# Other byte offsets for the activation tiles of a hybrid encoder layer

## The chip, the cores and the metric

The kernel runs on one core of one Trainium2 chip. The metric is the time of one execution in microseconds (us). Its work on the engines is told by their names in the profile: PE (TensorE, matmuls), PEld (TensorE's loads of the stationary operand), DVE (VectorE), ACT (ScalarE), POOL (GpSimd) and SP, which only issues transfers here.

## The reference

One encoder layer over 256 tokens of 2048 channels, in float32:

```python
h = rmsnorm(x, norm_mix_pre); z = h @ w_in            # 2048 -> 13312
conv_b, conv_c, conv_in, q, k, v, g_a, g_b = split(z)
y_a = (conv_b * conv3(conv_c * conv_in)) @ w_out_conv
y_b = attention(rope(rmsnorm(q)), rope(rmsnorm(k)), v) @ w_out_attn
mixed = (sigmoid(g_a + bias) * y_a + sigmoid(g_b + bias) * y_b) @ w_merge
x = x + rmsnorm(mixed, norm_mix_post)
h = rmsnorm(x, norm_mlp_pre)                          # then an MLP of 8192 hidden channels
x = x + rmsnorm(square(relu(h @ w_up)) @ w_down, norm_mlp_post)
```

There are 16 query heads and 4 key/value heads of 128 channels, with rotary positions.

## The kernel before, in words

Every float32 product is made of three matmuls: each operand is split into a high and a low float32r part (`split`, lines 74 to 81), and high times high, high times low and low times high are summed in PSUM. The weights come from HBM in pieces of 512 KB (`raw`); ACT writes their high part `whi` (L76), DVE their low part `wlo` (L77).

A layer of work is a matrix of 2048 by 512 weights against all 256 tokens, and it is done in one of two ways. `linear` (L152 to L154) holds 128 tokens as the stationary operand and moves 512 columns of weights: 96 matmuls a layer. `linear_channels` (L182, L186, L189) holds 128 by 128 weights and moves all 256 tokens: 192 matmuls a layer. So one text speaks of tokens that move, and of weights that move.

The split tokens lie in three large tiles of SBUF, each with a high and a low half, and `pair` (line 88) makes them:

- A: first the normalised input `hT` (moves in 12 convolution and 8 gate layers; stationary in the K, the V and 4 Q layers, where the weights move), later the hidden activations `fT` (stationary in the 16 layers of `down`).
- B: first `yT`, the convolution's output (moves in 4 layers), then `mT`, the merged branches (stationary in 4 layers of `merged`).
- C: first `oT`, the attention's output (moves in 4 layers), then `x2T`, the input of the MLP (stationary in the first of 16 `w_up` layers, which `hidden` does; moves in the other 15, `hidden_channels`).

The order is: K, V; four times Q, then three convolution layers with the attention of that group among them; gate A and `w_oc` layers in turn (8), gate B and `w_oa` layers in turn (8); 4 merge layers; and four times 4 layers of `w_up` and 4 of `w_down`. Matmuls are issued in this order on PE and nothing else is reordered by the change. The attention's own matmuls (L386 to L388) and the transposes (L231, L419, L584) are placed among the convolution layers by a list of due times (`later`, `tick`).

`LATE` gives the number of float32 elements by which a role's data start late in its tile; the tile is made longer by the largest of them. The pool `big` holds A, then M (keys and values, then the merged sum), then C, then B, one behind the other, and the weight buffers `raw`, `whi` and `wlo` come behind it. In bytes of a partition, A begins at 18112, M at 50944, C at 67328, B at 100096, `raw` at 133056; every `whi` and `wlo` buffer begins at 192 modulo 256, also those of the second ring that is added after the attention. The pieces that a matmul reads are multiples of 256 bytes apart from their tile's start, so a role has one distance modulo 256, and here it is given as that of the moving operand minus that of the stationary one:

| role | layers | distance before |
|---|---|---|
| A, tokens move (convolution, gates) | 20 | 64 |
| B, tokens move (`w_oc`) | 4 | 64 |
| C, tokens move (`w_oa`, `w_up`) | 4 + 15 | 64 |
| A, weights move (K, V, Q) | 6 | 192 |
| A, weights move (`w_down`) | 16 | 0 |
| B, weights move (merge) | 4 | 0 |
| C, weights move (first `w_up`) | 1 | 192 |

In the attention, scores (keys move against queries) have 64 and values (probabilities move against values) 192.

Of the kernel before, what the change touches and what calls it, by code (L numbers as in the profile page):

```python
# [10 lines left out]
F32R = mybir.dt.float32r  # L11
# [4 lines left out]
P = 128  # L16
# [16 lines left out]
def trunk_kernel(  # L33
# [30 lines left out]
    big = ctx.enter_context(tc.tile_pool(name="big", bufs=1))  # L64
# [18 lines left out]

    LATE = {"A": {True: 16, False: 0}, "B": {True: 0, False: 48}, "C": {True: 0}}

    def pair(tag, moving):

        n, at = 2 * KT * T, LATE[tag][moving]  # L90
        flat = big.tile([P, n + max(LATE[tag].values())], F32R, tag=tag, name=tag)
        both = flat[:, at : at + n].rearrange("p (h k t) -> p h k t", h=2, k=KT)
        return both[:, 0], both[:, 1]

# [181 lines left out]
    g_bias = ch[:, 5:7, :]  # L276

    hT = pair("A", True)

    def first_operands(k, n):  # L280
# [99 lines left out]
    )  # L380

    oT = pair("C", True)
    yT = pair("B", True)

    def mm3(acc, a, b, first, last):
# [363 lines left out]
```

## Time and profile before

| | us |
|---|---|
| median of 3 runs (1607.99 to 1609.61) | 1609.29 |
| the profiled execution, its own time | 1608.78 |
| its span, first to last instruction | 1607.0 |
| PE busy | 1594.8 |
| DVE busy | 948.0 |
| ACT busy | 710.0 |

A matmul's recorded duration overlaps the next one's, since they are pipelined. So the rate of PE is read from how many matmuls start in a stretch of time, and the duration only tells two rates apart. A view by stretches gives the busy time of PE and the number of its instructions; the number counts also those two or three that reach into the stretch at its edges.

### The profile page before, as it was taken

The page shows a single profiled execution, that of the slowest core. Times are in us where ns is not written, and L with a number is a line of the kernel's source. Part 1 is how long each engine was busy: PE and PEld are TensorE (multiplying, and loading weights), DVE is VectorE, ACT ScalarE, POOL GpSimd, SP SyncE. Part 2 cuts the span into 40 slices and gives each one's busy share as a digit, 9 for nine tenths or more (in the row PEclk, how much of TensorE's full clock was granted, in tenths as well). Part 3 has the DMA queues.
Part 4 walks back from the last instruction along what each step waited for, and adds up shares of the span by engine and source line. Part 5 has one row for each costly group of instructions (what it writes and reads, how often), then busy time and mean ns, then how long its engine had stood idle before and what let it go on. Part 6 is the DMA issues. An engine that isn't in the chain of part 4 may idle for free.

```text
span 1607.0 us, 26865 instructions
## 1 busy us (share of the span) xinstructions
PE 1594.8 (99%) x11210; PEld 1485.8 (92%) x11210; DVE 948.0 (59%) x1107; ACT 710.0 (44%) x860; POOL 35.7 (2%) x23
## 2 busy tenths in 40 slices
PE   9999999999999999999999999999999999999997
PEld 7799998999999999999988898899988998899986
DVE  6767676676765554555555865446655565555654
ACT  7444444444454443444444644444433344334441
POOL 0110100101000000000000000000000000000000
PEclk9999999999999999999999999999999999999999
DMA  8655546555476666666765666666666666656662
GB/s 316 199 178 158 184 137 204 173 168 183 152 251 193 192 189 204 191 195 194 247 207 163 200 190 194 197 192 186 183 199 191 188 186 191 192 183 195 186 207 85
DMA packets 86297, 306.28 MB, mean 191 GB/s; under 512 B 9632, under 2 KB 10016, under 8 KB 85920
## 3 DMA queue, kind: packets, MB, share of 16 engines
q1 hardware_dynamic: 84608, 300.32, 59.8%
q10 hardware_dynamic: 1568, 4.25, 0.8%
q8 instruction: 87, 1.43, 0.4%
q14 instruction: 34, 0.28, 0.1%
HBM read 302.44 MB, written 2.10 MB: 190 GB/s over the span
## 4 chain that ended last, share of the span: by engine, by line
PE 98%; DVE 1%; DMA 0%; POOL 0%; issue 0%; ACT 0%; SPq 0%; DVEq 0%; POOLq 0%; ACTq 0%
PE acc L182 20%; PE acc L189 20%; PE acc L186 20%; PE acc L153 12%; PE acc L154 12%; PE acc L152 12%; PE at L386 0%; PE at L387 0%; PE at L388 0%; PE tr L419 0%; DMA raw<-in_w_in 0%; PE tr L231 0%; POOL rs L243 0%; DVE wlo L77 0%; PE tr L584 0%
## 5 line engine op out<-in xcount | busy, mean ns | idle before, releaser
L77 DVE TENSOR_TENSOR wlo<-raw,whi 128x1024 fp32r<-128x1024 f32 (+1 forms) x561 | 684.9, 1223 | 583.9 <-ACT whi L76 582.2
L76 ACT CAST whi<-raw 128x1024 fp32r<-128x1024 f32 (+1 forms) x561 | 588.1, 1050 | 758.4 <-PE acc L186 385.0
L182 PE MATMUL acc<-A,whi 128*128 128x256 f32 x1280 | 357.1, 279 | 0.0
L186 PE MATMUL acc<-A,whi 128*128 128x256 f32 x1280 | 355.2, 278 | 0.0
L189 PE MATMUL acc<-A,wlo 128*128 128x256 f32 x1280 | 355.1, 277 | 0.0
L182 PE MATMUL acc<-C,whi 128*128 128x256 f32 x1216 | 339.5, 279 | 0.0
L189 PE MATMUL acc<-C,wlo 128*128 128x256 f32 x1216 | 338.7, 279 | 0.0
L186 PE MATMUL acc<-C,whi 128*128 128x256 f32 x1216 | 338.5, 278 | 0.0
L152 PE MATMUL acc<-whi,A 128*128 128x512 f32 x704 | 275.3, 392 | 1.7 <-ACT whi L76 1.7
L153 PE MATMUL acc<-wlo,A 128*128 128x512 f32 x704 | 276.1, 392 | 0.8 <-DVE wlo L77 0.8
L154 PE MATMUL acc<-whi,A 128*128 128x512 f32 x704 | 275.8, 392 | 0.0
L186 PEld LDWEIGHTS acc<-A,whi 128*128 128x128 f32 x1280 | 240.4, 188 | 0.2
L182 PEld LDWEIGHTS acc<-A,whi 128*128 128x128 f32 x1280 | 240.3, 188 | 0.2
L189 PEld LDWEIGHTS acc<-A,wlo 128*128 128x128 f32 x1280 | 240.1, 188 | 0.0
L189 PEld LDWEIGHTS acc<-C,wlo 128*128 128x128 f32 x1216 | 228.5, 188 | 0.0
L182 PEld LDWEIGHTS acc<-C,whi 128*128 128x128 f32 x1216 | 228.1, 188 | 0.2
L186 PEld LDWEIGHTS acc<-C,whi 128*128 128x128 f32 x1216 | 227.8, 187 | 0.2
L153 PEld LDWEIGHTS acc<-wlo,A 128*128 128x128 f32 x704 | 132.6, 188 | 30.4 <-DVE wlo L77 2.1
L152 PEld LDWEIGHTS acc<-whi,A 128*128 128x128 f32 x704 | 132.4, 189 | 30.4 <-ACT whi L76 2.5
L154 PEld LDWEIGHTS acc<-whi,A 128*128 128x128 f32 x704 | 132.7, 188 | 28.8
L182 PE MATMUL acc<-B,whi 128*128 128x256 f32 x256 | 70.7, 276 | 0.0
L186 PE MATMUL acc<-B,whi 128*128 128x256 f32 x256 | 70.7, 276 | 0.0
(144 smaller groups left out, 1113.7 us busy)
## 6 DMA issues: line engine op xcount, KB each, us to landing
raw<-in_w_in SPq DMA_DIRECT2D x207, 512.0 KB, 4.3
raw<-in_w_up SPq DMA_DIRECT2D x128, 512.0 KB, 3.6
raw<-in_w_dn SPq DMA_DIRECT2D x128, 512.0 KB, 3.8
raw<-in_w_oc SPq DMA_DIRECT2D x32, 512.0 KB, 4.4
raw<-in_w_oa SPq DMA_DIRECT2D x32, 512.0 KB, 4.2
raw<-in_w_mg SPq DMA_DIRECT2D x32, 512.0 KB, 4.3
xj<-in_x SPq DMA_DIRECT2D x4, 512.0 KB, 8.0
xr<-in_x ACTq DMA_DIRECT2D x1, 2048.0 KB, 9.8
```

Of the source, the lines that this page charges most:

```text
L76: nc.scalar.copy(hi, src)
L77: nc.vector.tensor_tensor(lo, src, hi.bitcast(F32), op=ALU.subtract)
L152: nc.tensor.matmul(accs[t], lhsT=ah[:, a, ts_], rhs=wh[:, g, :], start=first, stop=False)
L153: nc.tensor.matmul(accs[t], lhsT=ah[:, a, ts_], rhs=wl[:, g, :], start=False, stop=False)
L154: nc.tensor.matmul(accs[t], lhsT=al[:, a, ts_], rhs=wh[:, g, :], start=False, stop=last)
L182: nc.tensor.matmul(acc, lhsT=wh[:, g, cs], rhs=ah[:, a, :], start=a == 0 and c % 2 == 0, stop=False, skip_group_check=True,)
L186: nc.tensor.matmul(acc, lhsT=wh[:, g, cs], rhs=al[:, a, :], start=False, stop=False, skip_group_check=True)
L189: nc.tensor.matmul(acc, lhsT=wl[:, g, cs], rhs=ah[:, a, :], start=False, stop=a == KT - 1, skip_group_check=True)
```

## The change

The offsets in `LATE` change, and the size of a tile is rounded up to a multiple of 16 elements (64 bytes). Nothing else is edited.

```diff
-    LATE = {"A": {True: 16, False: 0}, "B": {True: 0, False: 48}, "C": {True: 0}}
+    LATE = {"A": {True: 32, False: 48}, "B": {True: 8, False: 8}, "C": {True: 0}}
...
         n, at = 2 * KT * T, LATE[tag][moving]
-        flat = big.tile([P, n + max(LATE[tag].values())], F32R, tag=tag, name=tag)
+        flat = big.tile([P, n + -(-max(LATE[tag].values()) // 16) * 16], F32R, tag=tag, name=tag)
```

A grows from 32832 to 32960 bytes, so M, C and B begin 128 bytes later; B shrinks from 32960 to 32832, so `raw` and the weight buffers stay where they are. The distances become:

| role | before | after |
|---|---|---|
| A, tokens move | 64 | 128 |
| B, tokens move | 64 | 224 |
| C, tokens move | 64 | 192 |
| A, weights move (K, V, Q) | 192 | 128 |
| A, weights move (`w_down`) | 0 | 64 |
| B, weights move (merge) | 0 | 32 |
| C, weights move (first `w_up`) | 192 | 64 |
| scores / values | 64 / 192 | 192 / 64 |

## Rows read from the trace of the kernel before

**Rows 1.** The page: busy time of the engines, and the chain by engine.

```profile
PE 1594.8 (99%) x11210; PEld 1485.8 (92%) x11210; DVE 948.0 (59%) x1107; ACT 710.0 (44%) x860; POOL 35.7 (2%) x23
...
PE 98%; DVE 1%; DMA 0%; POOL 0%; issue 0%; ACT 0%; SPq 0%; DVEq 0%; POOLq 0%; ACTq 0%
```

**Rows 2.** PE by stretches: start:end, length, busy (count), granted clock, DMA.

```profile
154.40:176.80 22.40, 22.40 (x99) 1.00 0.61 190
176.80:252.00 75.20, 75.20 (x650) 1.00 0.53 168
...
447.40:795.60 348.20, 348.20 (x3074) 1.00 0.65 207
795.60:860.90 65.30, 65.30 (x290) 1.00 0.65 203
885.80:910.10 24.30, 24.30 (x115) 1.00 0.51 163
910.10:978.80 68.70, 68.70 (x585) 1.00 0.69 215
979.00:1066.00 87.00, 87.00 (x386) 1.00 0.64 193
1066.00:1156.30 90.30, 90.30 (x769) 1.00 0.62 187
...
1421.00:1511.30 90.30, 90.30 (x768) 1.00 0.61 187
```

**Rows 3.** Groups of PE matmuls by line, 447.5 to 795: xcount, busy us, mean ns.

```profile
L182 PE MATMUL acc<-A,whi 128*128 128x256 f32 x512 | 141.3, 276 | 0.0
...
L182 PE MATMUL acc<-B,whi 128*128 128x256 f32 x256 | 70.7, 276 | 0.0
...
L182 PE MATMUL acc<-C,whi 128*128 128x256 f32 x255 | 70.4, 276 | 0.0
```

**Rows 4.** The same view, 1066.2 to 1156: w_up layers of the second quarter.

```profile
L189 PE MATMUL acc<-C,wlo 128*128 128x256 f32 x255 | 71.1, 279 | 0.0
L186 PE MATMUL acc<-C,whi 128*128 128x256 f32 x255 | 71.1, 279 | 0.0
L182 PE MATMUL acc<-C,whi 128*128 128x256 f32 x254 | 71.1, 280 | 0.0
```

**Rows 5.** PE in order of time (start us, us): attention values at 220.21.

```profile
220.21 0.29 PE L386 MATMUL at<-ph,kv 128*128 128x256 f32 x1
220.33 0.28 PE L387 MATMUL at<-pl,kv 128*128 128x256 f32 x1
220.45 0.28 PE L388 MATMUL at<-ph,kv 128*128 128x256 f32 x1
220.56 0.28 PE L386 MATMUL at<-ph,kv 128*128 128x256 f32 x1
220.68 0.28 PE L387 MATMUL at<-pl,kv 128*128 128x256 f32 x1
220.79 0.28 PE L388 MATMUL at<-ph,kv 128*128 128x256 f32 x1
220.90 0.28 PE L386 MATMUL at<-kv,qh 128*128 128x256 f32 x1
```

**Rows 6.** The same view: attention values at 122.21.

```profile
122.21 0.28 PE L386 MATMUL at<-ph,kv 128*128 128x256 f32 x1
122.33 0.28 PE L387 MATMUL at<-pl,kv 128*128 128x256 f32 x1
122.45 0.28 PE L388 MATMUL at<-ph,kv 128*128 128x256 f32 x1
122.56 0.28 PE L386 MATMUL at<-ph,kv 128*128 128x256 f32 x1
122.68 0.28 PE L387 MATMUL at<-pl,kv 128*128 128x256 f32 x1
122.80 0.28 PE L388 MATMUL at<-ph,kv 128*128 128x256 f32 x1
```

**Rows 7.** The chain in order of time (start us, us): one group of transposes.

```profile
93.16 0.44 PE tr L231 x4
```

**Rows 8.** PE, PEld, DVE, ACT, POOL by stretches: gate stage, second quarter of w_up.

```profile
447.40:795.60 348.20, 348.20 (x3074) 348.20 (x3074) 189.38 (x179) 156.92 (x173) 0.00 (x0) 1.00 0.65 207
...
1066.00:1156.30 90.30, 90.30 (x769) 90.30 (x768) 50.36 (x52) 37.06 (x40) 0.00 (x0) 1.00 0.62 187
```

## The prediction, made before the result was known

> **What bounds the kernel now.** I read the page first: PE is busy 1594.8 of 1607.0 us, and 98% of the chain is PE [rows 1]. DVE and ACT stand at 59% and 44%. So the time is the number of matmuls times the interval at which PE starts them, and the change touches only the addresses that these matmuls read. The next view is therefore PE by stretches, one stretch for each stage, with the matmuls that the code puts there [rows 2]. I divide length by number.
>
> Where 256 tokens move: the gate stage holds 16 layers of 192, 3072 matmuls in 348.2 us, **113.3 ns** each. A quarter of w_up holds 768 in 90.3 us, **117.6 ns**, a difference of 4.3 ns. Where 512 columns of weights move: four layers of down hold 384 in 87.0 us, **226.6 ns**; three layers of merge 288 in 65.3 us, 226.7 ns; but one Q layer holds 96 in 22.4 us, **233.3 ns**. The granted clock is 1.00 of 2.4 GHz in all of these, so it is not the clock. The views by line say the same with durations: 276 ns for A, B and C in the gate stage [rows 3], 279 to 280 ns for C in w_up [rows 4].
>
> What the reader should see is that there are two rhythms for each kind of layer, about 4% and 3% apart, and that they are held for whole stages. For weights that move, the two go with the distance: 0 (down, merge) is the quicker, 192 (Q) the slower. For tokens that move, the distance is 64 throughout, and both rhythms occur; even the same tile C is quick against w_oa and slow against w_up. So at 64 the distance doesn't decide it; what came before does. The stage that begins behind a layer with moving weights (convolution behind Q, w_up behind down) begins slow, and the gate stage, which follows a convolution that had already gone over, stays quick for 3072 matmuls.
>
> One place shows tokens-sized matmuls at another distance: the attention's values, at 192, in 16 blocks of 6. In 12 of them the starts go as at 220.21: intervals of 0.12, 0.12, and then 0.11, 0.12, 0.11, 0.11, and what follows is quick [rows 5]. In 4 of them they stay at 0.12 all through, as at 122.21 [rows 6]. At 192 a slow beginning is thus mostly left within two matmuls, whereas w_up at 64 keeps it for 768.
>
> **The change part by part.** No instruction, transfer or wait is added or taken; the list of PE, ACT, DVE and SP is the same. All of the effect is an interval times a count. The price of a rhythm: 4.3 ns x 192 = 0.83 us for a layer of moving tokens, (233.3 - 226.6) x 96 = 0.64 us for one of moving weights.
>
> 1. *C, tokens move, w_up: 64 to 192.* 15 layers, 2880 matmuls, slow now. The nearest rows are the values' blocks at this very distance, of which 12 of 16 go quick [rows 5, 6]. If they hold: 2880 x 4.3 ns = 12.4 us gained. The other end is 0, the slow rhythm kept (no row of a worse one in a stage without stalls). I take the gain.
>
> 2. *A, tokens move, convolution: 64 to 128.* A group of three layers with its attention takes 75.2 us [rows 2]. It holds 576 + 48 matmuls and six groups of transposes at 0.44 us [rows 7]: all quick it would be 624 x 113.3 ns + 2.6 = 73.3 us, all slow 76.0. So two thirds of it are slow now, and the four groups can gain 4 x 1.9 = 7.6 us or lose 4 x 0.8 = 3.2. 128 lies midway between 64, which keeps what it is given, and 192; I take half of the gain, 3.8 us. Scores and values change places at 64 and 192: 192 matmuls in all, under 0.9 us either way, within this.
>
> 3. *A, B and C in the gate stage: 64 to 128, 224 and 192.* Quick now. Bounds: 0 gained (no row of a quicker one), 16 x 0.83 = 13.3 us lost. 224 is nearest to 192, 128 is between two distances at which the quick rhythm was seen; I take 0.
>
> 4. *Weights move: down 0 to 64, merge 0 to 32.* Quick now, 16 and 4 layers; bounds 0 and 10.2 + 2.6 = 12.8 us lost. Both new distances are nearer to 0 (226.6 ns) than to 192 (233.3 ns); I take 0, the least certain of my choices.
>
> 5. *Weights move: K, V, Q 192 to 128; first w_up 192 to 64.* Slow now: 6 layers, bounds 0 and 3.9 us gained; 128 is nearer to 192, I take 0. The first w_up layer, by the same rule, gains 0.6.
>
> *Does something else become late?* A quicker w_up layer asks for its weights 4% sooner. The gate stage runs at the quick rate already with DVE at 189 of 348 us and ACT at 157, and no PE wait; w_up needs DVE 50.4 of 90.3 and ACT 37.1 [rows 8]. Scaled to 87.0 us that is 58% and 43%, so the cover holds. A write of ACT or DVE that starts 32 or 64 bytes elsewhere has no row of its own; with DVE at 59% [rows 1] a few per cent more would not reach PE.
>
> Sum: 12.4 + 3.8 + 0.6 = 16.8 us gained. The profiled execution took 1608.8 us (span 1607.0 and 1.8 around it), so 1592.0; the median of the runs is 0.5 above the profiled one, which makes **1592.5 us**.
>
> **The rivals.**
>
> *No effect.* The rhythm is set by history alone, at any distance. For it: w_oa and w_up differ at one tile and one distance [rows 3, 4]. Against it: down and merge are quick in every layer and Q slow in each of four. Then the time is 1609, within 1606 to 1613. The Trainium skill speaks for this one: "TensorE: Matmul & The Clock Gate", in its steps of a matmul, says that the moving operand and the load of the stationary one have read ports of their own, so that loading the next weights takes nothing from the running matmul. By that the distance between the two could not matter and the sum would be zero; the rows for down against Q do not agree with it, unless something besides the distance separates those layers.
>
> *Tokens quick, weights slow.* Down at 64 and merge at 32 go as Q does at 192: the 16.8 us less 12.8, 1609 - 4 = 1605. For it: only 0 was ever seen quick, and 64 and 192 mirror each other about 0. Against it: no row.
>
> *Slower: the held rhythm is broken.* The gate stage is quick because one distance, 64, runs through 3072 matmuls, and nothing disturbs a rhythm once it is there. With 128, 224 and 192 in turn, each of its 16 layers begins at a jump of distance, as at 122.21, where the quick matmuls before a jump from 64 to 192 became slow [rows 6]. If the jump is lost every time: 13.3 us; w_up then starts slow as now, and if the convolution stays at its mixture that gives 1622, and with down slow as well 1635. It decides as soon as more gate layers start slow than w_up layers turn quick.
>
> **How the numbers follow.** About 0.2% (3.2 us) is what a measurement of this kernel can tell from none. The forecast has 0.42, with its own range from 1583 (all convolution, K, V and Q quick too) to 1600; no effect 0.18; tokens quick and weights slow 0.14; slower 0.26. The likeliest gives 1592.5. For 8 in 10 I go down to 1582, all that the rows allow at the quick rhythm, and up to 1623, the break of the gate stage without that of down. Faster: 0.42, 0.11 of the third case and 0.03 of the second, 0.56. Same: 0.16. Slower: 0.28.
>
> **What would show it.** In the profile of the changed kernel: a quarter of w_up in 87.0 us instead of 90.3, with 276 ns durations, shows step 1 right; the group of three convolution layers at 73.3 to 75.2 step 2; the gate stage at 348.2 step 3, and 361.5 the slower rival; four layers of down at 87.0 step 4, and 89.6 its opposite; a Q layer at 22.4 step 5, 21.8 if it gains. An interval below 113.3 or 226.6, or above 117.8 or 233.3, in a stage without waits would mean that there are more than two rhythms and that my bounds are wrong.

## The result, and the profile after

| | before | after |
|---|---|---|
| median of the runs, us | 1609.29 | 1617.63 (1617.41 to 1620.76) |
| ratio after to before, 95% interval | | 1.006 [1.0037, 1.0083] |
| profiled execution, us (span) | 1608.78 (1607.0) | 1617.63 (1615.9) |

The change made the kernel slower by 0.6%, inside the range given, but the forecast was 1592.5, on the other side. On the page, PE still bounds the kernel; its busy time rose by about as much as the span.

```profile
PE 1603.0 (99%) x11210; PEld 1489.1 (92%) x11210; DVE 947.3 (59%) x1107; ACT 710.7 (44%) x860; POOL 32.4 (2%) x23
...
PE 98%; DVE 1%; DMA 0%; POOL 0%; issue 0%; ACT 0%; SPq 0%; DVEq 0%; POOLq 0%; ACTq 0%
```

PE by stretches (columns as in [rows 2]): a Q layer; three convolution layers with their attention; the whole gate stage; in it one layer each of gate A (A at 128), w_oc (B at 224), w_oa (C at 192), gate B (A at 128); three merge layers; the first w_up layer, the rest of that quarter, four w_down layers and the next quarter of w_up.

```profile
154.60:176.90 22.30, 22.30 (x98) 1.00 0.60 186
176.90:253.50 76.60, 76.60 (x649) 1.00 0.52 166
451.20:811.50 360.30, 360.30 (x3075) 1.00 0.63 199
451.20:474.00 22.80, 22.80 (x195) 1.00 0.77 259
474.00:496.70 22.70, 22.70 (x194) 1.00 0.66 205
656.00:677.80 21.80, 21.80 (x194) 1.00 0.59 188
677.80:700.60 22.80, 22.80 (x195) 1.00 0.62 189
811.50:878.70 67.20, 67.20 (x290) 1.00 0.64 198
903.60:928.10 24.50, 24.48 (x118) 1.00 0.50 161
928.10:994.50 66.40, 66.40 (x585) 1.00 0.72 222
994.50:1082.40 87.90, 87.90 (x386) 1.00 0.64 192
1082.40:1169.40 87.00, 87.00 (x769) 1.00 0.64 194
```

Beside [rows 2]: w_up went from 90.3 to 87.0 us a quarter, as hoped, and the gate stage from 348.2 to 360.3, which was not. The groups of matmuls by line in the gate stage show where (beside [rows 3]): A and B rose from 276 to 281 ns, C stayed at 276.

```profile
L183 PE MATMUL acc<-A,whi 128*128 128x256 f32 x512 | 144.1, 281 | 0.0
...
L183 PE MATMUL acc<-B,whi 128*128 128x256 f32 x256 | 71.9, 281 | 0.0
...
L183 PE MATMUL acc<-C,whi 128*128 128x256 f32 x255 | 70.4, 276 | 0.0
```

Summed from first start to first start over the layers of each kind, from the two traces:

| | change, us |
|---|---|
| w_up, 15 layers | -12.5 |
| gate A and gate B layers (A at 128), 8 | +8.2 |
| convolution with attention, 12 | +5.1 |
| w_oc (B at 224), 4 | +3.8 |
| w_down (64), 16 | +3.3 |
| merge (32), 4 | +2.3 |
| K, V, Q (128) and first w_up (64) | -1.4 |
| w_oa (C at 192), 4 | +0.1 |
| sum | +8.9 |

The spans differ by 8.9. Of the 1.4 us gained in the layers at 128 and 64, 0.8 lie in K, the first layer, which took 25.4 and 27.3 us in the traces of experiments 9 and 10, where its addresses are those of before; so they can't be put down to the edit.

### The profile page after: what moved, and what is told of

Same layout as the page of the kernel before. It is cut to its first block, busy times and chain, and to the rows that moved or that the text cites. A ratio compares the mean times of both kernels' runs of the same rounds, so it can differ in the third digit from the quotient of the medians.

```text
span 1615.9 us, 26865 instructions
## 1 busy us (share of the span) xinstructions
PE 1603.0 (99%) x11210; PEld 1489.1 (92%) x11210; DVE 947.3 (59%) x1107; ACT 710.7 (44%) x860; POOL 32.4 (2%) x23
## 4 chain that ended last, share of the span: by engine, by line
PE 98%; DVE 1%; DMA 0%; POOL 0%; issue 0%; ACT 0%; SPq 0%; DVEq 0%; POOLq 0%; ACTq 0%
PE acc L183 20%; PE acc L190 20%; PE acc L187 20%; PE acc L155 12%; PE acc L154 12%; PE acc L153 12%; PE at L387 0%; PE at L388 0%; PE at L389 0%; PE tr L420 0%; DMA raw<-in_w_in 0%; PE tr L232 0%; POOL rs L244 0%; DVE wlo L77 0%; PE tr L585 0%
## 5 line engine op out<-in xcount | busy, mean ns | idle before, releaser
L183 PE MATMUL acc<-A,whi 128*128 128x256 f32 x1280 | 362.2, 283 | 0.0
L190 PE MATMUL acc<-A,wlo 128*128 128x256 f32 x1280 | 360.3, 282 | 0.0
L187 PE MATMUL acc<-A,whi 128*128 128x256 f32 x1280 | 360.2, 281 | 0.0
L155 PEld LDWEIGHTS acc<-whi,A 128*128 128x128 f32 x704 | 132.4, 188 | 27.3
L190 PE MATMUL acc<-B,wlo 128*128 128x256 f32 x256 | 71.9, 281 | 0.0
L183 PE MATMUL acc<-B,whi 128*128 128x256 f32 x256 | 71.9, 281 | 0.0
## 6 DMA issues: line engine op xcount, KB each, us to landing
xr<-in_x ACTq DMA_DIRECT2D x1, 2048.0 KB, 10.2
```

Of the source, the lines that this page charges most:

```text
L155: nc.tensor.matmul(accs[t], lhsT=al[:, a, ts_], rhs=wh[:, g, :], start=False, stop=last)
L183: nc.tensor.matmul(acc, lhsT=wh[:, g, cs], rhs=ah[:, a, :], start=a == 0 and c % 2 == 0, stop=False, skip_group_check=True,)
L187: nc.tensor.matmul(acc, lhsT=wh[:, g, cs], rhs=al[:, a, :], start=False, stop=False, skip_group_check=True)
L190: nc.tensor.matmul(acc, lhsT=wl[:, g, cs], rhs=ah[:, a, :], start=False, stop=a == KT - 1, skip_group_check=True)
```

## The experiments

The tokens' distances are set by `LATE`; in the kernels below the sizes are given by themselves, so that the weight buffers can be held in place (against the kernel before):

```diff
-        flat = big.tile([P, n + max(LATE[tag].values())], F32R, tag=tag, name=tag)
+        flat = big.tile([P, n + MORE[tag]], F32R, tag=tag, name=tag)
```

Each was timed beside the kernel before on the same chip (medians 1607.65 to 1607.76).

**1. All moving tokens at 192, w_down and merge back at 0.**

```diff
+    LATE = {"A": {True: 48, False: 0}, "B": {True: 0, False: 16}, "C": {True: 0}}
+    MORE = {"A": 48, "B": 16, "C": 0}
```

> All tokens that move at distance 192 (A, B, C), fT and mT back at 0, K/V/Q and the first w_up at 64. Theory 1 (the distance of a layer sets its interval; 192 is quick for moving tokens, as C shows in the changed kernel): w_up, gates, w_oc, w_oa and the convolution all at 113.3 ns, 21.8 us a layer; K, V, Q at 228.9 ns, 22.0 us; w_down and merge at 226.7 ns; 12.6 + 7.3 + about 3 us less than before: 1586 us (1583 to 1590). Theory 2 (the quick rhythm is handed over from the layer before, and w_up became quick because w_down at 64 now precedes it): with w_down back at 0, w_up is slow again at 22.6 us a layer: about 1599 us.

Measured: 1602.84 us, ratio 0.9968 [0.9956, 0.9981]. By stretches: gate stage, four w_down layers, and the w_up quarter behind them.

```profile
442.20:790.40 348.20, 348.20 (x3075) 1.00 0.66 207
973.10:1060.20 87.10, 87.10 (x386) 1.00 0.65 193
1060.20:1150.70 90.50, 90.50 (x770) 1.00 0.62 187
```

At 192 the gate stage is quick (113.3 ns) and w_up slow (117.8): one distance, two rhythms, as 64 had before. Theory 1, at 1586, fails in w_up; theory 2, at 1599, comes nearer. The convolution with its attention took 74.8 us a group, 1.5 more than the 73.3 of an all quick one that both counted on.

**2. The changed kernel with A at 64 where it moves.**

```diff
-    LATE = {"A": {True: 32, False: 48}, "B": {True: 8, False: 8}, "C": {True: 0}}
+    LATE = {"A": {True: 16, False: 48}, "B": {True: 8, False: 8}, "C": {True: 0}}
```

> The changed kernel with A undone where its tokens move: 64 again, all else as changed (so K, V, Q are at 192 again). Theory 1: the convolution returns to its mixture (75.2 us for three layers with attention instead of about 77), Q to 22.4 us; gate layers at 64 keep the rhythm that they are given: 21.8 us behind C at 192, and 21.8 or 22.6 behind B at 224, which stays at 22.7; in all 1605 to 1612 us. The rival of the prediction (a jump of distance between layers breaks the rhythm): every gate layer slow at 22.6 us or more, 1613 us or more.

Measured: 1621.29 us in one run, slower than the whole change: far above theory 1, and with every gate layer slow, as the rival said. Gate stage, four w_down layers, the next w_up quarter:

```profile
449.30:811.50 362.20, 362.20 (x3074) 1.00 0.64 199
996.40:1086.10 89.70, 89.70 (x388) 1.00 0.63 188
1086.10:1173.10 87.00, 87.00 (x769) 1.00 0.64 194
```

All 16 layers of the gate stage are slow, w_oa at 192 too (22.6 us). Going back to the address of before did not bring back the rate of before. It was not a jump that broke it, however: the first gate layer has the distance of the convolution in front of it, and the convolution already ended slow. Its last stretch here, and in the kernel before:

```profile
435.00:449.00 14.00, 14.00 (x122) 1.00 0.76 252
433.90:446.90 13.00, 13.00 (x117) 1.00 0.81 259
```

That is about 118 and 113 ns a matmul. The attention's values among these layers stand at 64 here and at 192 before, since M lies 128 bytes later; whether that made the difference was not tested. And this quarter of w_down, at 64, ran at 233.3 ns, while later ones in the same trace ran at 228.9: weights that move have two rhythms at 64 as well.

**3. Tokens in place (but for the merge), weights and all that lies behind them moved by 128 bytes.**

```diff
+    LATE = {"A": {True: 16, False: 0}, "B": {True: 0, False: 0}, "C": {True: 0}}
+    MORE = {"A": 16, "B": 16, "C": 0}
```

> The tokens of A, B (first role) and C at the bytes where they were before the change; the weight buffers begin 128 bytes earlier instead. Distances: 192 for all moving tokens; K, V, Q, merge and the first w_up 64; w_down 128. Theory 1 (the difference counts): w_up, convolution and gate stage at 113.3 ns, 21.8 us a layer; K, V, Q and merge 22.0; w_down 22.3 us (232 ns), 8.6 us lost there; about 1596 us. Theory 3 (the tokens' own place modulo 256 counts, not the difference): w_up stays at 22.6, w_down at 21.8, Q at 22.4: 1609 us.

Measured: 1627.31 us in one run; neither. Gate stage; w_down at 128; the w_up quarter behind it.

```profile
443.90:805.70 361.80, 361.80 (x3074) 1.00 0.63 199
988.70:1078.00 89.30, 89.30 (x387) 1.00 0.64 189
1078.00:1168.40 90.40, 90.40 (x769) 1.00 0.62 187
```

w_down changed to 232.3 ns though its tokens had not moved, as A at 128 did in K, V and Q of the changed kernel; so the difference counts, against theory 3. But at 192 the gate stage was now slow all through, and w_up slow behind w_down at 128: the difference alone doesn't decide. The first experiment has the same distance in every layer from K to the last of the gate stage, and there the gate stage took 348.2 us and Q 228.9 ns a matmul, here 361.8 and 233.3. Up to there the two kernels differ in the addresses themselves; whether these or the instant at which a layer begins made the difference stays open.

**4. All moving tokens at 128.**

```diff
+    LATE = {"A": {True: 32, False: 0}, "B": {True: 0, False: 32}, "C": {True: 0}}
+    MORE = {"A": 32, "B": 32, "C": 0}
```

> All moving tokens at one distance, 128, so no jump between the layers of the gate stage; w_down and merge at 0. Theory 1: every layer of moving tokens as A's in the changed kernel, 22.8 us (118.7 ns) in the gate stage and w_up, 22.95 in the convolution; K, V, Q 22.3; about 1631 us. The rival of the prediction (jumps break the rhythm, a constant distance holds it): the gate stage holds 21.8 us a layer once it is quick, about 1614 us.

Measured: 1635.3 us in one run. Gate stage and a w_up quarter:

```profile
452.00:816.50 364.50, 364.50 (x3074) 1.00 0.63 197
1087.30:1179.40 92.10, 92.10 (x769) 1.00 0.60 184
```

A constant distance did not make the gate stage quick: 364.5 us is 118.7 ns. And w_up at 128 behind w_down at 0 took 120.0 ns. At 128 there are two rhythms too, and both are worse than either at 64 or 192.

**5. As the first, with w_down at 64.** `"A": {True: 48, False: 48}`, the rest as there.

> As the first experiment (moving tokens at 192), but w_down at 64 as in the changed kernel. Theory 2 (at 192 and at 64 both rhythms can be held and the layer before hands one over; w_down at 64 hands over the quick one): w_up at 21.8 us a layer in all four quarters, w_down 22.0 instead of 21.8: 12.1 us less and 3.4 more than the first experiment, about 1594 us. Theory 1 in what is left of it (something else than w_down made w_up slow there): w_up stays at 22.6, about 1606 us.

Measured: 1595.11 us, ratio 0.9925 [0.9911, 0.9938], against 1594 expected. Four w_down layers and the w_up quarter behind them:

```profile
970.50:1058.40 87.90, 87.90 (x386) 1.00 0.65 192
1058.40:1145.40 87.00, 87.00 (x769) 1.00 0.63 194
```

Nothing of w_up was edited against the first experiment; what lies in front of these three later quarters was. In the first quarter even that is the same: no matmul up to its end has another address than in the first experiment. Yet its third and fourth layers were slow there and quick here, 45.2 and 43.6 us for 384 matmuls:

```profile
927.90:973.10 45.20, 45.20 (x386) 1.00 0.63 188
926.90:970.50 43.60, 43.60 (x387) 1.00 0.65 196
```

The layer before these is broken twice by a group of four transposes (L231 of the kernel before). In time order it goes into the second group quick in both kernels, at 113 to 114 ns, and comes out slow in the first experiment and quick in this one. So four transposes can turn the rhythm too, and the addresses in front do not tell which way; one trace of each can't say whether it goes the same way every time. The kernel of this experiment is the best of all versions run, and beats both kernels.

**6. The kernel before with B and C alone as changed.**

```diff
+    LATE = {"A": {True: 16, False: 0}, "B": {True: 8, False: 8}, "C": {True: 32}}
+    MORE = {"A": 16, "B": 16, "C": 32}
```

> The kernel before with only B (224, and 32 in the merge) and C (192) as changed; A, its role in w_down, the keys and values and the attention's own distances stay. The convolution is as before, and the first gate layer begins quick at 64. The rival of the prediction (a jump of distance breaks a held rhythm): B's layers at 224 take 22.7, and the gate layers behind them, though at 64, stay slow at 22.6; C at 192 then too: about 1623 us with merge at 22.4. If each layer finds its own rhythm again: gate layers at 21.8 behind 224, C at 21.8: about 1615 us. In both w_up stays slow behind w_down at 0.

Measured: 1620.68 us in one run. The first gate layer (A, 64), the first w_oc layer (B, 224), the second gate layer (A, 64), the first w_oa layer (C, 192):

```profile
446.50:468.30 21.80, 21.80 (x195) 1.00 0.78 259
468.30:491.00 22.70, 22.70 (x195) 1.00 0.69 222
491.00:513.60 22.60, 22.60 (x195) 1.00 0.58 185
649.60:672.20 22.60, 22.60 (x195) 1.00 0.61 187
```

This is the course of the prediction's slower rival: the quick rhythm at 64 comes in from the convolution, ends at the first jump, and does not return for the remaining seven gate layers, though their addresses are those of before. But B at 224 is slow itself, so a rhythm broken by the jump and one taken over from a slow layer look alike here.

**7. and 8. Other distances.** In 7: `"A": {True: 8, False: 0}, "B": {True: 40, False: 0}, "C": {True: 16}`, MORE 8, 40, 16. In 8: `"A": {True: 40, False: 0}, "B": {True: 24, False: 0}, "C": {True: 0}`, MORE 40, 24, 0.

> A look at other distances: moving tokens A 32, B 0, C 96; moving weights K/V/Q 224, w_down 0, merge 160, first w_up 160. If a quick rhythm for moving tokens exists only around 64 and 192 (128 and 224 showed none): 22.6 us or more a layer for A at 32 and B at 0; C at 96 lies 32 from 64 and from 128, 21.8 or 22.7. For moving weights 0 stays at 226.7 ns, and 160 and 224 at 232 to 234 like 32, 128 and 192. If neighbours of 0 are quick also for moving tokens, A and B at 21.8.

> A look at other distances: moving tokens A 160, B 0, C 160; moving weights K/V/Q and merge 96, w_down 0, first w_up 96. If the quick rhythm is only around 64 and 192: A and C at 160, which is 32 from 192 and from 128, between 21.8 and 22.8 us, the same in both; B at 0 22.6 or more; 96 for moving weights between 64 (228.9 ns) and 128 (232.3 ns). If w_down at 0 hands over a slow rhythm at any distance: C slow in w_up but perhaps quick against w_oa.

Measured: 1634.38 and 1631.36 us, one run each. Of the first: the first gate layer and a later one, A at 32; w_oc B at 0; w_up C at 96; three merge layers at 160.

```profile
447.00:469.40 22.40, 22.40 (x194) 1.00 0.77 251
492.50:515.10 22.60, 22.60 (x194) 1.00 0.57 185
515.10:538.20 23.10, 23.10 (x195) 1.00 0.59 185
1086.30:1178.50 92.20, 92.20 (x770) 1.00 0.61 184
812.10:879.50 67.40, 67.40 (x289) 1.00 0.63 196
```

Of the second: a gate layer and a w_up quarter, both at 160, and Q at 96.

```profile
542.00:564.50 22.50, 22.50 (x195) 1.00 0.61 188
1086.40:1177.60 91.20, 91.20 (x770) 1.00 0.61 186
154.00:176.40 22.40, 22.40 (x99) 1.00 0.59 188
```

0 came as expected, and so did 32 but for the first gate layer and the convolution in front of it, which ran at 116.7 ns. 96 missed (120.0 ns, as slow as 128 at its worst), and so did 96 for moving weights (233.3 ns, not between 228.9 and 232.3). 160 lay where it was expected, but was not the same everywhere: 117.4 ns in most of the gate stage, 118.7 in w_up. The guess that a distance behaves like the nearest one, on which the prediction stood, fails here.

**9. and 10. Six matmuls behind w_down, no address changed.**

```diff
+        if q < 3:
+            kick = ps_tr.tile([P, T], F32, name="tr")
+            for i in range(6):
+                nc.tensor.matmul(kick, lhsT=x2T[0][:, i, :P], rhs=fT[0][:, i, :], start=True, stop=True)
```

> The kernel before, no address changed, with 6 matmuls of 256 columns added behind each of the first three quarters of w_down: fT moves (192 modulo 256), x2T is stationary (0), distance 192, the pattern of the attention's values; their product goes unused. Theory 2 (at one distance both rhythms can be held, and what lies between two stages decides which): as 12 of 16 blocks of values did, these turn the slow rhythm into the quick one, and the three quarters of w_up behind them run at 21.8 us a layer instead of 22.6: 12 x 0.85 = 10.2 us less, 18 x 0.114 = 2.1 more, 1601 us beside 1609. Theory 1 (addresses alone set the interval): w_up stays at 22.6, 1611 us.

> The control: the same 18 matmuls at the same place with the operands exchanged (x2T moves, fT is stationary, distance 64, as in w_up itself and as in the attention's scores, behind which the rhythm of the trace before never changed from slow). Both theories: w_up stays at 22.6 us a layer, 1611 us. A quick w_up here as well would mean that any break does it, whatever its distance.

Measured: 1609.83 us, ratio 1.0013 [1.0003, 1.0023], and 1609.7, ratio 1.001 [1.0, 1.0019]. In both w_up stayed at 22.6 us a layer. For the first that is a miss of theory 2 as it was put. In time order, its block takes 0.71 us from its start to the next matmul (118 ns each), slow from the first one on, and w_up behind it is slow:

```profile
1064.16 0.87 PE L691 MATMUL tr<-A,C 128*128 128x256 f32 x6
1064.87 0.28 PE L182 MATMUL acc<-C,whi 128*128 128x256 f32 x1
```

It is what the first experiment had shown: behind w_down at 0, 192 begins slow. The 12 blocks of values that turned had been entered from the slow rhythm at 64 (two of the four that did not turn quick had been so as well).

**11. The same six matmuls inside w_up.** They stand behind the first 24 matmuls of the quarter, so that they are entered as those values were; `kickm` is a spare tile at 192, written once.

```diff
+        nc.scalar.copy(kickm, rstd2_row)
...
+    kickm = late.tile([P, T], F32R, name="kickm")
+
+    def kick():
+        tr = ps_tr.tile([P, T], F32, name="tr")
+        for i in range(6):
+            nc.tensor.matmul(tr, lhsT=x2T[0][:, i, :P], rhs=kickm, start=True, stop=True)
...
+        if q < 3:
+            later(1, kick)
```

> The kernel before, no address changed, with 6 extra matmuls of 256 columns inside the first w_up layer of the second, third and fourth quarter, behind its first 24 matmuls: a spare tile at 192 modulo 256 moves, x2T (0) is stationary; the product goes unused. Their distance is 192 and they are entered from the slow rhythm at 64, as the 12 blocks of values were that turned it (the earlier kick was entered from w_down at 0 and stayed slow from its first matmul, as w_up at 192 behind w_down at 0 did). Theory 2: intervals of 124, 118, 113 and so on inside the block, then w_up at 113.3 ns: the three quarters at 21.8 us a layer but for the start, 12 x 0.85 = 10 us less and 18 x 0.114 = 2 more, 1600 us beside 1608. If distance alone sets the interval: w_up stays at 22.6, 1610 us.

Measured: 1601.22 us, ratio 0.996 [0.9945, 0.9974], against 1600 expected. In time order around the block, and the whole quarter with it (774 matmuls) by stretches:

```profile
1067.03 0.28 PE L182 MATMUL acc<-C,whi 128*128 128x256 f32 x1
1067.15 0.28 PE L186 MATMUL acc<-C,whi 128*128 128x256 f32 x1
1067.27 0.28 PE L189 MATMUL acc<-C,wlo 128*128 128x256 f32 x1
1067.38 0.86 PE L685 MATMUL tr<-kickm,C 128*128 128x256 f32 x6
1068.07 0.28 PE L182 MATMUL acc<-C,whi 128*128 128x256 f32 x1
1068.19 0.28 PE L186 MATMUL acc<-C,whi 128*128 128x256 f32 x1
1068.30 0.28 PE L189 MATMUL acc<-C,wlo 128*128 128x256 f32 x1
1068.42 0.28 PE L182 MATMUL acc<-C,whi 128*128 128x256 f32 x1
```

```profile
1064.60:1152.30 87.70, 87.70 (x775) 1.00 0.62 192
```

Intervals of 0.12 before the block and 0.11 to 0.12 behind it, and over the quarter 87.7 / 774 = 113.3 ns. [Rows 4] had 279 to 280 ns at these very addresses. Six matmuls of 0.69 us together turned the 744 that follow. The other two quarters with a block turned as well. This settles that at 64 the rhythm is kept from what came before and not set by the addresses of the layer. That the distance of the block matters is not shown: none at another distance stood at this place, and transposes turn the rhythm too (experiment 5).

**12. The best version with B as changed.** `"B": {True: 8, False: 8}` in the fifth experiment's kernel.

> The best version so far (moving tokens at 192, w_down at 64) with B put back to what the change gives it: 224 where it moves, 32 in the merge. B's own layers at 224 take 22.7 us instead of 21.8 (4 x 0.95 = 3.8 us) and merge 22.4 instead of 21.8 (2.6). If 192 finds the quick rhythm again behind a slow layer, as C did in the changed kernel behind A at 128: the gate layers between them stay at 21.8, 1601.5 us. If the jump breaks it for good, as at 64 in the run with B and C alone: 7 gate and 4 w_oa layers at 22.6 too, 9.4 us more, 1611 us.

Measured: 1604.24 us, ratio 0.9977 [0.9967, 0.9986]. A w_oc layer at 224 and the gate layer at 192 behind it:

```profile
465.70:488.40 22.70, 22.70 (x194) 1.00 0.68 216
488.40:510.20 21.80, 21.80 (x195) 1.00 0.61 190
```

192 finds the quick rhythm again behind 224, unlike 64 in experiment 6. The stages differ from experiment 5 as expected (w_oc +3.8, merge +2.4, gates +0.1); the profiled run was another 2.0 us longer in K, its first layer, which no edit touched. The median is 2.7 above the 1601.5 expected and 2.1 above the profiled run, and the ten runs spread from 1599.6 to 1606.63; what sets the longer ones apart the one trace can't show.

## Why the prediction was wrong

**What bounds the kernel** was read rightly: only intervals changed. So was the warning that history counts at 64; experiment 11 shows it without any change of address, and experiments 1 and 5 show it at 192 too. The rival "no effect" is dead: no layer whose tokens move at 128 or 224 was quick in any run. The Trainium skill's "TensorE: Matmul & The Clock Gate", in "Step-by-step: what each phase is for", says that loading the next weights takes no SBUF read bandwidth from the running matmul. By the prediction's working the sum would then be zero; the gate stage, which went from 348.2 to 360.3 us, does not agree with that, though no run shows that the loads are what takes the time.

**Step 1** (w_up to 192) held: 12.4 us forecast, 12.5 measured. But the reason was only half right, and the size was in part luck. Six matmuls of values at 192 stood for the distance; 192 is slow behind w_down at 0 (experiment 1) and quick behind w_down at 64 (experiment 5). So 10.2 of the 12.5 us, those of the later three quarters, came because step 4's edit, which I had priced at nothing, handed the quick rhythm over. The values' blocks had been misread too. Of the 16, 14 were entered slow and 12 of these turned quick, but the two that were entered quick turned slow (as at 122.21), and behind 4 of the 12, where transposes follow, the matmuls were slow again. These rows showed that a block can turn the rhythm, and not that 192 is quick.

**Step 3** (the gate stage) is the step that failed: 0 taken, 12.1 lost. I took 224 and 128 to hold a quick rhythm because quick ones were seen at distances on both sides. Neither shows one in any layer of any run: 118.3 ns at 224, 118.7 to 120.0 at 128. The price was within its bound of 13.3, but only because C at 192 stayed quick: a gate layer at 128 lost 1.02 us, more than the 0.83 taken for the worst.

**Step 2** (convolution) failed for the same reason and beyond its bound: 3.8 gained was taken, 3.2 lost the worst, 5.1 lost measured. 128 has its own intervals, 118.7 ns here (120.0 in most of the first layer), above the 117.6 that I held to be the slow end. The prediction's own sign for that, an interval above 117.8, came: there are more than two rhythms.

**Step 4**: 0 taken, 5.6 lost, and nearest to 0 was the wrong rule: merge at 32 went to 233.3 ns (the price of Q, 2.3 us in all), w_down at 64 to 228.9, an interval that the trace of before didn't have. **Step 5**: 0.6 taken, 1.4 gained, of which 0.8 are K's and may have nothing to do with the edit.

**The slower rival** gave the sign, at 1622. Its course, a held rhythm that is lost and does not come back, is real (experiment 6), but it is not what happened here: in the changed kernel C at 192 is quick between slow layers of A. A and B lost by their own distances, and the jump was not needed. Putting A back to 64 in the changed kernel made it worse, since 64 then inherited the slow rhythm from the convolution: experiment 2.

What the runs leave open: why these distances and not others, and why one block or break turns the rhythm and another doesn't. What was seen, in whole layers:

| distance | tokens move, ns | weights move, ns |
|---|---|---|
| 0 | 120.0 | 226.7 |
| 32 | 116.7 or 117.8 | 233.3 |
| 64 | 113.3 or 117.8 | 228.9 or 233.3 |
| 96 | 120.0 | 233.3 |
| 128 | 118.7 or 120.0 | 232.3 |
| 160 | 117.4 or 118.7 | 234.3 |
| 192 | 113.3 or 117.8 | 233.3 |
| 224 | 118.3 | 233.4 |

## What to carry to other kernels

When a matmul-bound kernel shows the same instruction at two intervals, sort the layers by address and by what ran before them, before giving either the credit: here each distance allowed one or two rhythms, and what ran before chose, by a rule that these runs do not give. Do not interpolate between measured distances; measure the one that is to be used, behind the layer that will stand in front of it. And when one role's address is moved, count also the layers that inherit its rhythm.

## What was not expected of the hardware

A rhythm lasts for as long as nothing disturbs it: 3072 matmuls in the gate stage of before at 113.3 ns, 768 at 117.8 with the same distance, both at a granted clock of 1.00. Of 256 columns the quick interval is 113.3 ns and of 512 it is 226.7, twice that, at 0, where PEld was busy in 72.0 of the 87.0 us of a quarter of w_down in the kernel before; no distance gave less.
